# When the next generator in a lane of side work may begin: at its own due time, or as soon as the one ahead of it is through

## The chip, the cores and the metric

The kernel runs on one core of one Trainium2 chip. The metric is the device time of one execution in microseconds; before the change it is 2041.46 us, the median of three runs (2041.38, 2041.46 and 2047.03). The profile shown below is of one further execution, which took 2036.54 us.

The engines are named as the profile names them: PE is TensorE (matmuls and transposes), DVE is VectorE, ACT is ScalarE, POOL is GpSimd and SP is SyncE, which here only issues DMA transfers. Each engine takes its instructions in the order in which they were written, and waits where an operand is not there yet.

## The reference

Two transformer blocks run one after the other on 512 tokens of 1024 features, all in float32. Cut to what matters here:

```
# block 1
x  = x + gate_a * (concat(gla(h), pool(h)) @ w_out)       # w_out: 1024 x 1024
h2 = modulate(rmsnorm(x), ...)
logits = h2 @ [w_router_group, w_router_expert]            # 36 columns
x  = x + gate_m * moe(h2)                                  # 32 experts, two per token
x  = rmsnorm(x)
# block 2, layer A: gated delta rule, 8 heads of 128, chunks of 64 tokens
q, k, v, z, b, a = split(rms_norm(x) @ w_in)
q, k, v = silu(causal_depthwise_conv(q | k | v))           # 4 taps
q, k    = l2_norm(q), l2_norm(k)                           # per head and token
beta = sigmoid(b);  g = -exp(a_log) * softplus(a + dt_bias)
g_cum = cumsum(g in chunks)
a_low = strictly_lower((k * beta) @ k.T * decay(g_cum))
sol   = solve(I + a_low, [v * beta, k * beta * exp(g_cum)])
... scan over the chunks; o = rms_norm(o) * silu(z);  x = x + o @ w_out
x = x + swiglu(rms_norm(x))
# layer B: stick-breaking attention on shared k and v, then swiglu again
```

## The kernel before

The activations lie transposed in SBUF, features on the partitions and all 512 tokens on the free axis. A float32 product is made of three matmuls of halves: the high part of the weights (`ah`, from `whi`) and the low part (`al`) by the high part of the activations, and the high by the low. The profile shows these three as `mm<-ah,whi`, `mm<-al,whi` and `mm<-ah,wlo`, each 128x512. They are the main work of TensorE. `fm_pair` (from L509) makes two output tiles of a projection from 48 such matmuls. The last matmul of a tile is followed at once by an eviction, which `evict` issues (a `scalar_tensor_tensor` or `tensor_tensor` on VectorE, from PSUM to SBUF).

Everything else that a stage needs is side work. It is written as Python generators, and between each group of three matmuls `fm_pair` calls `tick` (L464), which lets side work issue a piece. The side work is kept in eight lanes, called A, I, B, J, C, V, W and X (L408). A lane is a queue of generators: the first of them runs, in pieces, and each piece ends with a `yield`. While it writes the program the kernel keeps an estimate of when each engine would be free and when each tile would be written (`Clock`, `Engine`). Two numbers follow from it for each lane. `add` (L420) stores with a generator the estimated time at which its input is there, `at`. `ready[lane]` is the estimated time at which what the last piece of that lane issued is finished. The larger of the two is the lane's due time:

```
def due(s, lane):
    q = s.lanes[lane]
    return max(s.ready[lane], q[0][1]) if q else 1e30
```

`tick` goes through the lanes and calls `step` once for each lane whose due time is not later than TensorE's estimated time. `until` and `drain`, which empty lanes where a phase ends or a tile is needed, take the lane with the smallest due time instead. `step` (L424) takes the next piece of the lane's first generator. If that generator turns out to have no further piece, it is taken off the queue and the loop goes on with the next generator in the same call. All this is done while the program is written. On the chip there is only the resulting order of instructions on each engine.

Two stretches of the program use the lanes in the way that matters here.

The second half of the out-projection of block 1 (`out(j, 1)`, from L1221; 281 to 320 us in the trace) has eight output tiles, k = 0 to 7. Eviction k (`xT<-mm,modT,xT` on VectorE) adds two generators. `router_gen(k)` in lane C issues the four router matmuls `lC<-wrg,xT` that read the evicted tile. `rows_gen(k)` in lane X issues four transposes `lA<-cst,xT` of it, then a copy on ScalarE (`rows<-lA`), and for k = 3 and 7 a store. The eviction is also squared (`nsq`, ScalarE) and summed (`nacc`, VectorE). `lA<-ones,nacc` on TensorE reads the sum after the last tile. The MoE follows.

The gated delta-net (`gdn`, from L1738; from 597 us) projects k, b and a, q, v and z in the order of `GDN_ORDER`: k0, ba, k1, k2, k3, q0, v0, q1, v1, q2, v2, q3, v3, z0 to z3, where each of these but ba is a pair of heads and 48 matmuls. Each evicted head (`xm<-mm,Rc`, VectorE) goes through `conv_gen` in lane V or W: one tap on ScalarE, three on VectorE (`kF<-xm,vbT,kF`, `qF<-...`, `vf<-...`, 128x512), and a silu on ScalarE. When that is done, it adds a generator to lane C. For a k or q head this is `norm_gen`: a square on ScalarE (`cs<-kF`), its sum on TensorE (`lC<-ones,cs`), and small work on VectorE (`kss`, `qss`). For a v head it is `v_gen`: four transposes `lC<-cst,vf` on TensorE, and `vb<-lC,rho` on VectorE. `gates_gen`, in lane C too, makes beta and the decays of all heads: `lC<-cst,baf`, some small work on VectorE and ScalarE (`beta`, `gm`), then `lC<-gm,cst` on TensorE. `lower` (lanes I and B) makes the triangular matrices from them (`lB<-ub,gm`, `E`, `lB<-kF`). `solve` (lane J) inverts their 32x32 blocks on VectorE in 30 steps of two instructions (`sub<-mt`, `mt<-mt,sub`), and gives way after each four steps. Its result goes through memory (`inv`) to `levels` in lane I (`lB<-inverted,XTs`).

On ScalarE the functions of exp and ln are in one table and silu in another. Where a function of the other table comes next, an ACT_TABLE_LOAD is issued.

Of the kernel before, what the change touches and what calls it, by code (L numbers as in the profile page):

```python
# [263 lines left out]
class Stream:  # L264
# [77 lines left out]
    def next(s, key):  # L342
        i = s.nn
        assert s.items[i][0] == key, (s.items[i][0], key)
        s.nn += 1
        if i - 1 in s.held:
            s.release(*s.held.pop(i - 1))
        with s.K.aside():
            s.split_to(i + 2)
            s.load()  # L350
        return s.hl.pop(i)
# [43 lines left out]
class Kern:  # L395
# [28 lines left out]
    def step(s, lane):  # L424

        q = s.lanes[lane]
        main = s.cur
        while q:
            gen, at = q[0]
            s.cur = max(s.ready[lane], at)  # L430
            try:
                due = next(gen)
            except StopIteration:
                q.pop(0)
                continue
            s.ready[lane] = s.cur + (due or 0.0)
            s.cur = main
            return True
        s.cur = main
        return False  # L440
# [863 lines left out]
    def moe(s):  # L1304
# [103 lines left out]
        tt(out=gates[:, 1], in0=gates[:, 0], in1=e2, op=OP.mult)  # L1408
        place0, step = sm("place0", [4]), sm("step", [4])
        tt(out=step, in0=oh[:, :, 1], in1=oh[:, :, 3], op=OP.add)  # L1410
        ts_(out=place0, in0=step, scalar1=-32.0, scalar2=64.0, op0=OP.mult, op1=OP.add)
        ts_(out=step, in0=place0, scalar1=-2.0, scalar2=None, op0=OP.mult)

        cnt, more, cap = sm("cnt", [NE]), sm("more", [NP]), sm("cap", [NP, 2])
# [1105 lines left out]
```

## Time and profile before

| | |
|---|---|
| median of three runs | 2041.46 us |
| profiled execution | 2036.54 us |
| its span (first to last instruction) | 2034.8 us |
| mean granted clock of TensorE | 0.973 |
| PE busy | 1952.2 us (96%), 10717 instructions |
| PEld busy (weight loads, beside PE) | 1471.0 us (72%) |
| DVE busy | 984.7 us (48%) |
| ACT busy | 750.9 us (37%) |
| POOL busy | 376.0 us (18%) |

The share of busy time says which engine could set the time. The timeline of that engine, instruction by instruction, says where it stood still, and the entry in brackets at the end of a row says for how long and which engine's instruction released it. Nearly all instructions carry the line L231, the helper through which every operation is issued, so that they are told apart by the names of the tiles they write and read.

### The profile page before, as it was taken

What the parts mean: (1) busy time and instruction counts of PE and PEld (TensorE: products, weight loads), DVE (VectorE), ACT (ScalarE), POOL (GpSimd) and SP (SyncE); (2) the same over time, 40 slices, a digit from 0 to 9 for tenths busy, and PEclk for the clock granted to TensorE, in tenths of its full rate; (3) what the DMA queues carried; (4) which work ended last, traced back from release to release, by engine and by line L of the source; (5) the groups of instructions that cost most, each with busy time, mean ns of one, the idle gap of its engine ahead of it and who ended that gap; (6) DMA issues with size and microseconds to landing.
All of it is one profiled execution on the core that took longest, in us unless ns stands there. A gap on an engine that the chain in (4) does not pass through costs nothing.

```text
span 2034.8 us, 26780 instructions
## 1 busy us (share of the span) xinstructions
PE 1952.2 (96%) x10717; PEld 1471.0 (72%) x10717; DVE 984.7 (48%) x1612; ACT 750.9 (37%) x1184; POOL 376.0 (18%) x305
## 2 busy tenths in 40 slices
PE   7999997999997998999999999999999989999999
PEld 4766775344445776888788888888888768888887
DVE  3445433343447679445554433445665544433432
ACT  3443422222235543334343222224666542322322
POOL 1423202112105342122121100101121221100110
PEclk9989997999999998999999999999999999999999
DMA  9213376999951323101223332323211123333332
GB/s 315 75 44 125 113 271 243 421 415 401 404 198 55 110 78 95 46 22 42 87 87 100 97 100 93 94 88 109 73 63 51 54 73 95 98 98 94 93 93 73
DMA packets 175368, 268.86 MB, mean 132 GB/s; under 512 B 24301, under 2 KB 148457, under 8 KB 162697
## 3 DMA queue, kind: packets, MB, share of 16 engines
q1 hardware_dynamic: 152784, 249.28, 35.5%
q10 hardware_dynamic: 19784, 13.40, 2.2%
q0 software_dynamic: 2672, 4.44, 0.6%
q8 instruction: 86, 1.41, 0.3%
q14 instruction: 42, 0.34, 0.1%
HBM read 263.41 MB, written 7.86 MB: 133 GB/s over the span
## 4 chain that ended last, share of the span: by engine, by line
PE 73%; DVE 6%; ACT 2%; issue 1%; POOL 0%; ACTq 0%; DMA 0%; DVEq 0%; POOLq 0%
PE mm L231 57%; PE lA L231 9%; PE lB L231 7%; DVE qF L231 1%; DVE kF L231 1%; DVE sub L231 1%; PE lC L231 1%; DVE xT L231 1%; DVE mt L231 0%; DVE vf L231 0%; ACT ah L231 0%; DVE wlo L231 0%; DVE al L231 0%; DVE nacc L231 0%; ACT whi L231 0%
## 5 line engine op out<-in xcount | busy, mean ns | idle before, releaser
L231 PE MATMUL mm<-ah,whi 128*128 128x512 f32 (+1 forms) x1232 | 503.5, 409 | 0.6 <-DVE xT L231 0.5
L231 PE MATMUL mm<-al,whi 128*128 128x512 f32 (+1 forms) x1232 | 487.9, 396 | 8.6 <-DVE al L231 8.5
L231 PE MATMUL mm<-ah,wlo 128*128 128x512 f32 (+1 forms) x1232 | 487.4, 396 | 0.8 <-DVE wlo L231 0.8
L231 DVE TENSOR_TENSOR wlo<-wraw,whi 128x1024 fp32r<-128x1024 f32 (+3 forms) x174 | 216.1, 1244 | 289.3 <-ACT whi L231 287.9
L231 ACT ACTIVATE whi<-wraw 128x1024 fp32r<-128x1024 f32 (+2 forms) x212 | 214.7, 1014 | 327.8 <-PE mm L231 172.1
L231 PEld LDWEIGHTS mm<-ah,whi 128*128 128x128 f32 (+1 forms) x1232 | 234.3, 190 | 60.4 <-issue 8.9
L231 PEld LDWEIGHTS mm<-al,whi 128*128 128x128 f32 (+1 forms) x1232 | 234.2, 190 | 59.5 <-DVE al L231 11.4
L231 PEld LDWEIGHTS mm<-ah,wlo 128*128 128x128 f32 (+1 forms) x1232 | 233.9, 190 | 54.0 <-DVE wlo L231 2.0
L231 POOL TENSOR_TENSOR sg<-sg,fR 128x512 f32<-128x512 f32 x44 | 57.0, 1298 | 525.5 <-ACT sg L231 525.5
L231 POOL TENSOR_TENSOR wlo<-wraw,whi 128x1024 fp32r<-128x1024 f32 x38 | 94.2, 2480 | 247.8 <-ACT whi L231 242.1
L231 PE MATMUL mm<-hidh,whi 128*128 128x512 f32 x352 | 139.2, 395 | 0.0
L231 PE MATMUL mm<-hidh,wlo 128*128 128x512 f32 x352 | 138.0, 392 | 0.0
L231 PE MATMUL mm<-hidl,whi 128*128 128x512 f32 x352 | 136.6, 388 | 0.0
L231 PE MATMUL mm<-slot,moex 128*32 128x512 f32 (+1 forms) x1024 | 116.8, 598 | 0.1
L231 ACT ACTIVATE moex<-lA,modP,g2P 128x128 f32<-128x128 f32 x64 | 27.5, 455 | 161.1 <-PE lA L231 145.8
L231 PEld LDWEIGHTS mm<-slot,moex 128*32 128x32 f32 x1024 | 31.6, 110 | 71.4 <-issue 64.1
L231 PEld LDWEIGHTS mm<-hidh,wlo 128*128 128x128 f32 x352 | 66.1, 188 | 15.5
L231 PEld LDWEIGHTS mm<-hidl,whi 128*128 128x128 f32 x352 | 66.1, 188 | 14.5
L231 PEld LDWEIGHTS mm<-hidh,whi 128*128 128x128 f32 x352 | 66.2, 188 | 13.0
L231 DVE TENSOR_TENSOR xT<-mm,xT 128x512 f32<-128x512 f32 x64 | 44.0, 687 | 56.2 <-PE mm L231 51.0
L231 ACT ACTIVATE hidh<-fu 128x512 fp32r<-128x512 f32 x44 | 27.8, 633 | 104.3 <-DVE fu L231 104.3
L231 POOL TENSOR_TENSOR nacc<-nacc,nsq 128x512 f32<-128x512 f32 x28 | 39.5, 1409 | 144.7 <-ACT nsq L231 144.7
(552 smaller groups left out, 3104.8 us busy)
## 6 DMA issues: line engine op xcount, KB each, us to landing
slot<-in_w_e_in_dram SPq DMA_DIRECT2D x64, 1024.0 KB, 12.2
wraw<-in_w_gu_dram SPq DMA_DIRECT2D x88, 512.0 KB, 3.4
slot<-in_w_e_out_dram SPq DMA_DIRECT2D x32, 1024.0 KB, 13.3
wraw<-in_w_down_dram SPq DMA_DIRECT2D x40, 512.0 KB, 3.4
wraw<-in_w_ada_dram SPq DMA_DIRECT2D x32, 512.0 KB, 4.1
wraw<-in_gdn_w_in_dram SPq DMA_DIRECT2D x32, 512.0 KB, 3.8
wraw<-in_w_kv_dram SPq DMA_DIRECT2D x16, 512.0 KB, 3.3
wraw<-in_w_in_dram SPq DMA_DIRECT2D x14, 512.0 KB, 4.6
```

The lines of the kernel that those rows point to most:

```text
L231: r = f(*a, **k)
```

## The change

In `step`, when a generator has no further piece and is taken off its lane's queue, the lane now goes on with the next one in the same call only if that generator's own due time is not later than TensorE's estimated time. Otherwise `step` returns, and the next generator begins at a later `tick`, when its time has come.

```
             except StopIteration:
                 q.pop(0)
+                s.cur = main
+                if q and s.due(lane) > s.nc.tensor.t:
+                    return True
                 continue
```

The rule holds for all lanes and the whole program. The order that comes out differs in two stretches alone, the two described above; the rest reads the same on every engine. TensorE, VectorE, GpSimd and SyncE have as many instructions as before, and SyncE's order is unchanged. ScalarE has 1282 instead of 1278. The four that are added are ACT_TABLE_LOADs, all in the gated delta-net.

The first of three places is TensorE in the out-projection of block 1, at the eviction of tile 0, where the router matmuls and the transposes of this tile stand.

```order
L231 MATMUL mm<-ah,whi 128x512
L231 MATMUL mm<-al,whi 128x512
L231 MATMUL mm<-ah,wlo 128x512
L231 MATMUL lC<-wrg,xT 128x36 x4
L231 MATMUL mm<-ah,whi 128x512
L231 MATMUL mm<-al,whi 128x512
L231 MATMUL mm<-ah,wlo 128x512
L231 MATMUL lA<-cst,xT 128x128 x4
```

After the change:

```order
L231 MATMUL mm<-ah,whi 128x512
L231 MATMUL mm<-al,whi 128x512
L231 MATMUL mm<-ah,wlo 128x512
L231 MATMUL mm<-ah,whi 128x512
L231 MATMUL mm<-al,whi 128x512
L231 MATMUL mm<-ah,wlo 128x512
L231 MATMUL lC<-wrg,xT 128x36 x4
L231 MATMUL mm<-ah,whi 128x512
L231 MATMUL mm<-al,whi 128x512
L231 MATMUL mm<-ah,wlo 128x512
```

The router matmuls of a tile no longer stand right behind its last matmul; six matmuls of the next tile come between them, and the other tiles are moved in the same way or further.

The second place is VectorE at the start of the gated delta-net, where the taps of the first k heads (`kF`) and the gates (`beta`, `gm`) share the queue. Before the change:

```order
L231 TENSOR_TENSOR baf<-mm,Rc 16x512
L231 SCALAR_TENSOR_TENSOR kF<-xm,vbT,kF 128x512 x2
L231 TENSOR_SCALAR beta<-beta 128x32
L231 RECIPROCAL beta<-beta 128x32
L231 TENSOR_TENSOR gm<-lC,ab 128x32
L231 SCALAR_TENSOR_TENSOR gm<-gm,nbeta 128x32
L231 SCALAR_TENSOR_TENSOR gm<-gm,ab 128x32
L231 TENSOR_TENSOR gml<-gm,gmh 128x32
L231 SCALAR_TENSOR_TENSOR kF<-xm,vbT,kF 128x512 x3
```

After the change:

```order
L231 TENSOR_TENSOR baf<-mm,Rc 16x512
L231 SCALAR_TENSOR_TENSOR kF<-xm,vbT,kF 128x512
L231 TENSOR_SCALAR beta<-beta 128x32
L231 RECIPROCAL beta<-beta 128x32
L231 TENSOR_TENSOR gm<-lC,ab 128x32
L231 SCALAR_TENSOR_TENSOR gm<-gm,nbeta 128x32
L231 SCALAR_TENSOR_TENSOR gm<-gm,ab 128x32
L231 TENSOR_TENSOR gml<-gm,gmh 128x32
L231 SCALAR_TENSOR_TENSOR kF<-xm,vbT,kF 128x512 x2
L231 MEMSET xm 128x3
L231 TENSOR_TENSOR xm<-mm,Rc 128x512
L231 SCALAR_TENSOR_TENSOR kF<-xm,vbT,kF 128x512 x2
```

One tap instead of two stands ahead of `beta`, and an eviction stands among the taps behind `gml`.

The third place is VectorE near the end of the solve, where the last taps of a q head (`qF`) stand among the batches of `sub` and `mt`. Before the change:

```order
L231 SCALAR_TENSOR_TENSOR qF<-xm,vbT,qF 128x512 x2
L231 TENSOR_TENSOR sub<-mt 128x150
L231 TENSOR_TENSOR mt<-mt,sub 128x6x25
L231 TENSOR_TENSOR sub<-mt 128x130
L231 TENSOR_TENSOR mt<-mt,sub 128x5x26
L231 TENSOR_TENSOR sub<-mt 128x108
L231 TENSOR_TENSOR mt<-mt,sub 128x4x27
L231 TENSOR_TENSOR sub<-mt 128x84
L231 TENSOR_TENSOR mt<-mt,sub 128x3x28
L231 MEMSET xm 128x3
L231 TENSOR_TENSOR xm<-mm,Rc 128x512
```

After the change:

```order
L231 TENSOR_TENSOR sub<-mt 128x150
L231 TENSOR_TENSOR mt<-mt,sub 128x6x25
L231 TENSOR_TENSOR sub<-mt 128x130
L231 TENSOR_TENSOR mt<-mt,sub 128x5x26
L231 TENSOR_TENSOR sub<-mt 128x108
L231 TENSOR_TENSOR mt<-mt,sub 128x4x27
L231 TENSOR_TENSOR sub<-mt 128x84
L231 TENSOR_TENSOR mt<-mt,sub 128x3x28
L231 SCALAR_TENSOR_TENSOR qF<-xm,vbT,qF 128x512 x2
L231 MEMSET xm 128x3
L231 TENSOR_TENSOR xm<-mm,Rc 128x512
```

The last two taps now stand behind a batch of eight solve instructions that they stood ahead of.

How far TensorE's reading of a head stands behind the head's eviction, counted in main matmuls between the two in the program as written, is as follows. The instructions are those of lane C, and the heads count from 0 to 7.

| PE instruction | head | before | after |
|---|---|---|---|
| `lC<-gm,cst` (behind `lC<-cst,baf`) | all | 21 | 27 |
| `lC<-ones,cs` | k2 | 34 | 48 |
| `lC<-ones,cs` | k4 | 62 | 42 |
| `lC<-ones,cs` | q0 | 30 | 27 |
| `lC<-ones,cs` | q3 | 38 | 41 |
| `lC<-cst,vf` | v0 | 38 | 30 |

The first `lB<-kF` stands 18 matmuls behind the `lB<-ub,gm` of its matrices before, and 12 after. The `lC<-cst,vf` of the last two heads, v6 and v7, come 21 and 24 matmuls later in the program than before, with 9 instead of 6 matmuls between the two.

## Rows read from the trace of the kernel before

**Rows 1.** Busy time by window: PE, PEld, DVE, ACT, POOL; clock, DMA share, GB/s.
```profile
280.00:345.00 65.00, 51.91 (x317) 41.55 (x316) 27.71 (x80) 14.76 (x28) 11.22 (x27) 0.84 0.65 243
345.00:597.00 252.00, 250.59 (x1910) 105.59 (x1912) 102.75 (x184) 66.37 (x128) 37.88 (x28) 0.99 0.94 382
...
760.00:820.00 60.00, 51.49 (x260) 41.90 (x258) 53.97 (x102) 20.69 (x28) 14.24 (x6) 0.89 0.35 93
```

**Rows 2.** Timeline, TensorE, out-projection: start, duration, instruction, [idle before <-releaser].
```profile
288.08 0.39 PE L231 MATMUL mm<-al,whi 128*128 128x512 f32 x1
288.31 0.39 PE L231 MATMUL mm<-ah,wlo 128*128 128x512 f32 x1
289.54 1.08 PE L231 MATMUL lC<-wrg,xT 128*128 128x36 f32 x8 [0.84 <-DVE xT L231]
...
294.84 0.63 PE L231 MATMUL lA<-cst,xT 128*128 128x128 f32 x4 [0.94 <-DVE xT L231]
...
318.47 1.08 PE L231 MATMUL lC<-wrg,xT 128*128 128x36 f32 x8 [0.84 <-DVE xT L231]
...
320.01 0.69 PE L231 MATMUL lA<-ones,nacc 128*128 128x2 f32 x5
```

**Rows 3.** Timeline, VectorE, same stretch.
```profile
288.74 0.75 DVE L231 SCALAR_TENSOR_TENSOR xT<-mm,modT,xT 128x512 f32<-128x512 f32 x1 [3.27 <-PE mm L231]
...
319.17 0.69 DVE L231 TENSOR_TENSOR nacc<-nacc,nsq 128x512 f32<-128x512 f32 x1 [0.76 <-ACT nsq L231]
```

**Rows 4.** Timeline, SyncE's queue, before and into the MoE.
```profile
345.76 0.90 SPq L231 DMA_DIRECT2D slot<-in_w_e_out_dram  x2
```

**Rows 5.** Timeline, TensorE, GDN stage: the waits longer than one microsecond, and one slow matmul.
```profile
647.01 1.08 PE L231 MATMUL lC<-gm,cst 128*128 128x32 f32 x8 [2.36 <-DVE gm L231]
...
649.06 0.63 PE L231 MATMUL mm<-ah,whi 128*128 128x512 f32 x1
...
665.39 1.02 PE L231 MATMUL lC<-ones,cs 128*64 128x2 f32 x16 [2.92 <-ACT cs L231]
...
716.36 0.93 PE L231 MATMUL lC<-ones,cs 128*64 128x2 f32 x16 [1.44 <-ACT cs L231]
...
755.29 0.63 PE L231 MATMUL lC<-ones,cs 128*64 128x2 f32 x16 [1.68 <-ACT cs L231]
...
771.85 1.12 PE L231 MATMUL lC<-cst,vf 128*128 128x128 f32 x4 [2.78 <-ACT vf L231]
...
793.87 1.02 PE L231 MATMUL lC<-ones,cs 128*64 128x2 f32 x16 [5.74 <-ACT cs L231]
...
835.77 0.90 PE L231 MATMUL lC<-cst,vf 128*128 128x128 f32 x4 [3.50 <-ACT E L231]
```

**Rows 6.** Timeline, VectorE, GDN stage.
```profile
638.85 5.19 DVE L231 SCALAR_TENSOR_TENSOR kF<-xm,vbT,kF 128x512 f32<-128x512 f32 x2 [0.20 <-ACT kF L231]
643.96 1.25 DVE L231 TENSOR_SCALAR beta<-beta 128x32 f32<-128x32 f32 x1
...
652.67 0.74 DVE L231 SCALAR_TENSOR_TENSOR kF<-xm,vbT,kF 128x512 f32<-128x512 f32 x1
...
791.27 1.41 DVE L231 SCALAR_TENSOR_TENSOR qF<-xm,vbT,qF 128x512 f32<-128x512 f32 x2
792.60 0.30 DVE L231 TENSOR_TENSOR sub<-mt 128x150 f32<-128x150 f32 x1
...
794.83 0.24 DVE L231 TENSOR_TENSOR mt<-mt,sub 128x84 f32<-128x84 f32 x1
```

**Rows 7.** Timeline, GpSimd, beside the first of them.
```profile
638.28 5.20 POOL L231 TENSOR_TENSOR wlo<-wraw,whi 128x1024 fp32r<-128x1024 f32 x2 [8.80 <-ACT whi L231]
```

**Rows 8.** Timeline, ScalarE, GDN stage.
```profile
793.20 0.61 ACT L231 ACTIVATE cs<-qF 128x512 f32<-128x512 f32 x1
...
831.98 1.28 ACT L218 ACT_TABLE_LOAD   x1 [1.92 <-DMA inverted<-inv]
833.27 0.60 ACT L231 ACTIVATE eg<-lB 128x512 f32<-128x512 f32 x1
```

## The prediction

> **What bounds the kernel now.** I read the busy times first. TensorE is busy for 1952.2 of 2034.8 us, VectorE for about half of that. A change of order can only take away what TensorE stands still, some 80 us, and what it loses at a low clock beside that. The order differs in two stretches, so I then read the busy time by window to see how tight they are. From 345 to 597 us, in the MoE, TensorE is busy for 250.6 of 252 us and the DMA engines for 0.94 [rows 1]. From 760 to 820 us, in the delta-net's solve, VectorE is busy for 53.97 us and TensorE for 51.49 of 60 [rows 1]. There the two engines are both near their limit, and VectorE is the nearer. Last I read TensorE's timeline in the two stretches for its idle times and the instruction that ended each.
>
> **The out-projection.** Main matmuls start 0.23 us apart (288.08, 288.31), and the router matmuls behind the last of a tile start 1.23 us after it, at 289.54 [rows 2]. They wait for the eviction, which starts at 288.74 and takes 0.75 us [rows 3]. So such a place costs 1.0 us. There are four of them, at 289.54, 304.01, 312.86 and 318.47 us, each with an idle time of 0.84 us; a fifth is the transposes at 294.84, idle for 0.94, which costs 1.1 [rows 2]. After the change six matmuls, 1.4 us, stand between, more than the 1.0 us that is missing, and the eviction depends on nothing that moves. The first three and the fifth go: 3 × 1.0 + 1.1 = 4.1 us. The place at 318.47 is behind the last tile, where no matmul is left to fill it. The way to `lA<-ones,nacc` at 320.01 leads there through the eviction, the square and the sum at 319.17 [rows 2, 3] in any case, and it keeps its length. About 0.4 us is added to the gain by a set of transposes that moves from among the matmuls into this wait. The sum is −4.5 us, with ends at 0 and −5.
>
> Does it carry? The next transfer of an expert's weights that is issued after the first ones stands at 345.76 us [rows 4], behind work that hangs on the router, so that it starts earlier by what the router does. With TensorE without a gap in the MoE [rows 1], the whole of the stage shifts. I count the 4.5 us in full.
>
> **The delta-net, its start.** TensorE stands 2.36 us before `lC<-gm,cst` at 647.01, and after it eight matmuls show 0.63 us as that at 649.06 does, against 0.39 elsewhere [rows 2, 5]: 8 × 0.24 = 1.9 us at the low one of the two clocks (1.2 instead of 2.4 GHz), which followed the pause. The cause is VectorE. `beta` begins at 643.96, right behind two taps that took 5.19 us together from 638.85 [rows 6], while GpSimd did two `wlo` from 638.28 [rows 7]. Two taps alone take 1.41 us (791.27), so they lost 3.8 us to the overlap [rows 6]. After the change `beta` stands behind one of the two, that is some 2.6 us earlier, and `lC<-gm,cst` six matmuls (1.4 us) later. Together this is 4.0 us against a wait of 2.36; but the small instructions now meet the second `wlo`, which ends at 643.48 [rows 7], and then they start only 0.5 us earlier. I leave 0.5 us of the wait standing: −(2.36 + 1.9 − 0.5) = −3.8 us. The wait for the squares of k head 2 at 665.39 is 2.92 us [rows 5]; they stand 14 matmuls further behind their eviction, 3.2 us, but the taps that they wait for also have a pair of others moved in front of them (1.41). I take −1.2 us (ends 0 and −2.9). The start gives −5.0.
>
> **The middle.** At 716.36 TensorE waits 1.44 us and at 755.29 1.68 us [rows 5]. The squares of q0 and q3 stand 9 and 3 matmuls later in the program. For q0 the wait was on VectorE's queue, and 9 × 0.23 = 2.1 us cover it: −1.4. For q3 3 × 0.23 = 0.7, of which I take −0.5. The ends are 0 and −3.1 for both.
>
> **The solve.** Here VectorE decides. The wait of 2.78 us at 771.85 is for taps of v2 that stand behind the same two batches as before; it stays. The longest wait, 5.74 us at 793.87, is for `cs` at 793.20, behind the silu that follows the taps at 791.27 [rows 5, 6, 8]. These taps now stand behind one batch more. The batch runs from 792.60 to 795.07, so 2.5 us [rows 6], and the square is read three matmuls earlier (0.7): +3.2 us. If such a batch or its taps meet two more `wlo`, they lose 3.8 more, so the ends are 0 (VectorE has one eviction and two taps less among the batches, 0.68 + 2 × 0.7, and three `wlo` may fall otherwise) and +7.0.
>
> **Behind the solve.** TensorE waits 3.50 us at 835.77 for the bank of the transposes of v6 [rows 5]. VectorE frees it behind `E`, which needs `eg` at 833.27, behind a table load at 831.98 of 1.28 us [rows 8]. The transposes stand 24 matmuls later, 5.5 us. I take −3.0 (ends 0 and −3.5).
>
> **New waits.** The squares of k4 come 42 instead of 62 matmuls behind the eviction; k2 had 34 and waited 2.92, so at 8 × 0.23 more cover there remains 1.1. v0's transposes come after 30 instead of 38; q0 at 30 waited 1.44, and I take 1.0. The first `lB<-kF` lose 6 matmuls of cover, 1.4 us, half of it exposed: 0.7. Four more table loads on ScalarE are 4 × 1.28 = 5.1 us [rows 8], most of it beside waiting ScalarE time (busy 20.69 of 60 us in the solve's window [rows 1]); I take 0.2. New waits: +3.0, with ends at 0 and +9.
>
> On the table load the profile shows the next ScalarE instruction at 833.27, 0.01 us behind the load's end [rows 8]. The Trainium skill ("ScalarE: Activation LUTs", section "What ACT_TABLE_LOAD costs") puts a drain of 1380 ns on top of a load of 1283 ns, 2.66 us for each switch. By that rule four loads would come to 10.6 us instead of 5.1, and if they stood on the path the result would be slower. The trace here agrees with the load and shows no drain behind it.
>
> The sum: −4.5 − 5.0 − 1.9 + 3.2 − 3.0 + 3.0 = −8.2 us. From the profiled execution of 2036.54 this gives 2028.3. The median of the three runs lies 4.9 us above that execution, and the runs after will be compared with it, so I predict 2041.46 − 8.2 = 2033.
>
> **The rivals.**
> - *VectorE takes the delta-net's gain back.* Only the out-projection gains. In the solve's window VectorE is busy for 90% [rows 1]; whatever TensorE gains ahead of it, it waits for there, as long as VectorE's work starts no earlier. Against it: the start's gain brings the evictions forward too, and with them VectorE's work. −4.5, with +1 for what the moved batch costs: −3.5, 2038.
> - *All waits go.* The moved taps find VectorE free and GpSimd's `wlo` fall elsewhere. Then the out-projection gives 4.5, the start 2.4 + 1.9 + 2.9 = 7.2, the middle 3.1, the part behind the solve 3.5, with nothing new: −18.3, 2023. For it: each wait is short against the matmuls put before it. Against it: VectorE has no room in the solve.
> - *Slower: the late taps of q4.* The mechanism sits at 793.87. The taps moved behind the last full batch meet two `wlo` there, so that the wait grows by 3.2 + 3.8 = 7.0 us to some 13 us. The low clock follows it for eight matmuls, 1.9 us, as behind 647.01 [rows 5]. What the start and the middle gained is lost in this wait, since VectorE ends it, and the part behind the solve gives nothing, since two of the four added table loads (2 × 1.28 [rows 8]) then fall to the late q heads. The sum is 7.0 + 1.9 + 2.6 − 4.5 = +7.0, 2048. It decides from the point at which the wait at q4's squares is longer than 12 us. In favour: VectorE and GpSimd already meet for 3.8 us at 638.85 [rows 6, 7], and VectorE is the fuller engine here. Against: the moved taps are only two. Of such a meeting the Trainium skill ("SBUF — State Buffer", section "🔬 SBUF: two separate sides") says that GpSimd and a VectorE operation with two SBUF inputs take their shared ports for a whole instruction and block each other. By that rule a tap can lose up to a whole `wlo`, 2.6 us by the row [rows 7] instead of 1.9, and the sum would be +8.4; the 5.19 us for two taps agree with blocking.
>
> **How the numbers follow.** What a measurement of this kernel can tell from no change is about 0.3%, 6.1 us. The forecast, −8 with ±4, gets 0.46, and about 0.32 of it is beyond 6.1 us. The first rival gets 0.23 (−1 to −6.5), nearly all within, 0.03 beyond. The second gets 0.17, all faster. The third gets 0.14, of which 0.12 is beyond 6.1 us. So faster 0.52, same 0.36, slower 0.12. The range goes from 2019, the second rival with two more stretches at the full clock (2 × 1.9), to 2045: the forecast with the upper ends of the solve (3.8) and the new waits (6) and one more stretch at the low clock (1.9). It leaves out most of the third rival and a little beyond the second. The forecast's own range is 2029 to 2037.
>
> **What would show it.** Right: in the out-projection no idle time before `lC<-wrg,xT` save the last, and `lA<-ones,nacc` near 315.5 us; `lC<-gm,cst` with less than 1 us of wait and no slow matmuls behind it; the wait at q4's squares grown to about 9 us; the wait at the last `lC<-cst,vf` gone; the stages behind 900 us as long as before. Wrong: a wait of over 12 us at q4's squares or of over 2 us at k4's; a first wait for weights in the MoE; a delta-net that ends as late as before although its start was early; or a difference of more than 1 us between the parts that were not reordered.

## The result and the profile after

The kernel after takes 2032.48 us, the median of 11 runs (2020.68 to 2040.04), against 2041.38 us for the kernel before in 11 runs beside it (2034.91 to 2047.03). The ratio is 0.995, with a 95% interval from 0.9927 to 0.9972 (here and below it is taken over all runs, and not from the two medians). The medians differ by 9 us, the ratio comes to 10, and the interval goes from 6 to 15 us. The forecast of 2033 us and its sign hold. What stands behind the number is another matter for the delta-net, as the traces and the runs below show.

The page of the kernel after, its first two lines (span, then busy time, share and instructions of each engine):

```profile
span 2027.4 us, 26781 instructions
...
PE 1949.6 (96%) x10717; PEld 1468.5 (72%) x10717; DVE 981.0 (48%) x1612; ACT 756.3 (37%) x1188; POOL 373.8 (18%) x305
```

Here TensorE is as busy as before to within 3 us of 1952, and the four table loads are the 1188 instead of 1184 instructions of ScalarE. The span is 7.4 us shorter. TensorE's standing still, span less busy time, fell from 82.6 to 77.8 us, and nearly all of these 4.8 us are the out-projection's. In the delta-net it hardly changed, as will be seen.

The stages by window, in the kernel after (columns as in [rows 1]):

```profile
345.00:597.00 252.00, 249.48 (x1892) 105.96 (x1891) 100.18 (x182) 64.90 (x126) 38.92 (x29) 0.99 0.96 388
640.00:700.00 60.00, 56.70 (x351) 45.43 (x350) 46.18 (x94) 37.89 (x59) 23.77 (x13) 0.94 0.37 111
700.00:760.00 60.00, 57.80 (x361) 47.62 (x359) 46.69 (x93) 33.63 (x43) 29.94 (x15) 0.97 0.30 78
760.00:820.00 60.00, 47.73 (x243) 38.76 (x242) 51.66 (x103) 20.43 (x27) 12.62 (x5) 0.91 0.34 92
820.00:850.00 30.00, 28.81 (x214) 24.82 (x212) 15.31 (x29) 13.01 (x20) 6.48 (x4) 1.00 0.19 45
850.00:900.00 50.00, 47.94 (x363) 42.45 (x362) 24.50 (x61) 22.07 (x41) 9.30 (x7) 1.00 0.10 22
```

And the same windows of the kernel before, as far as [rows 1] does not have them:

```profile
640.00:700.00 60.00, 54.64 (x319) 44.78 (x318) 43.24 (x87) 35.15 (x55) 23.19 (x13) 0.91 0.36 108
700.00:760.00 60.00, 56.22 (x358) 46.45 (x357) 47.23 (x99) 30.02 (x41) 29.21 (x15) 0.94 0.30 77
820.00:850.00 30.00, 26.50 (x172) 22.95 (x171) 13.39 (x22) 9.50 (x15) 6.49 (x4) 0.94 0.19 45
850.00:900.00 50.00, 48.66 (x358) 43.87 (x357) 23.97 (x60) 18.57 (x36) 6.93 (x6) 0.93 0.07 11
```

The MoE is as tight as before [rows 1], 249.48 of 252 us. What differs in the delta-net is TensorE's granted clock, as a share of the full one, the third figure from the right: 0.91, 0.94, 0.89, 0.94 and 0.93 before, and 0.94, 0.97, 0.91, 1.00 and 1.00 after. TensorE's busy time in the solve's window even fell, from 51.49 to 47.73 us of 60.

TensorE in the out-projection, where the router's matmuls stand, after:

```profile
299.53 0.39 PE L231 MATMUL mm<-ah,wlo 128*128 128x512 f32 x1
299.75 0.97 PE L231 MATMUL lC<-wrg,xT 128*128 128x36 f32 x8
...
323.47 1.08 PE L231 MATMUL lC<-wrg,xT 128*128 128x36 f32 x8 [0.41 <-DVE xT L231]
...
325.01 1.02 PE L231 MATMUL lA<-ones,nacc 128*128 128x2 f32 x8
```

These are the router matmuls of tile 1, the ones at 289.54 in [rows 2]. (The place that is shown with the change as that of tile 0 is this one. Those of tile 0 stood six matmuls behind its last one before the change too, at 285.88, and did not wait.) They follow the main matmul ahead of them at the usual 0.22 us, where it was 1.23 [rows 2]. No others wait, nor do the transposes, save the last, which wait 0.41 us behind the eviction as they had to.

The delta-net's waits on TensorE, after:

```profile
652.09 0.97 PE L231 MATMUL lC<-gm,cst 128*128 128x32 f32 x8
...
661.93 1.02 PE L231 MATMUL lC<-ones,cs 128*64 128x2 f32 x16 [3.30 <-ACT cs L231]
...
748.06 0.63 PE L231 MATMUL lC<-ones,cs 128*64 128x2 f32 x16 [2.20 <-ACT cs L231]
...
775.84 1.11 PE L231 MATMUL lC<-cst,vf 128*128 128x128 f32 x4 [8.88 <-ACT vf L231]
...
783.20 0.63 PE L231 MATMUL lC<-cst,vf 128*128 128x128 f32 x4 [1.71 <-DVE vb L231]
...
794.39 0.63 PE L231 MATMUL lC<-ones,cs 128*64 128x2 f32 x16 [1.67 <-ACT cs L231]
```

Against [rows 5]: `lC<-gm,cst` no longer waits, and neither do k2, q0 and, behind the solve, the last v heads. In their place stand a wait of 3.30 us before k0's squares, which had none, one of 2.20 us at q2, where q3 had 1.68, one of 8.88 us at v2, where there were 2.78, and one of 1.71 us at v3. The wait at q4 fell from 5.74 to 1.67.

### The profile page after: what moved, and what is told of

Read it like the earlier page. It is cut to its first block, busy times and chain, and to the rows that moved or that the text cites. A ratio compares the mean times of both kernels' runs of the same rounds, so it can differ in the third digit from the quotient of the medians.

```text
span 2027.4 us, 26781 instructions
## 1 busy us (share of the span) xinstructions
PE 1949.6 (96%) x10717; PEld 1468.5 (72%) x10717; DVE 981.0 (48%) x1612; ACT 756.3 (37%) x1188; POOL 373.8 (18%) x305
## 3 DMA queue, kind: packets, MB, share of 16 engines
q8 instruction: 86, 1.41, 0.3%
## 4 chain that ended last, share of the span: by engine, by line
PE 73%; DVE 5%; ACT 2%; issue 2%; POOL 1%; DMA 0%; ACTq 0%; POOLq 0%; DVEq 0%
PE mm L231 57%; PE lA L231 9%; PE lB L231 7%; DVE sub L231 1%; DVE xT L231 1%; PE lC L231 1%; DVE qF L231 1%; DVE mt L231 0%; ACT ah L231 0%; DVE kF L231 0%; POOL wlo L231 0%; DVE vf L231 0%; DVE wlo L231 0%; DVE al L231 0%; ACT whi L231 0%
## 5 line engine op out<-in xcount | busy, mean ns | idle before, releaser
L231 DVE TENSOR_SCALAR moex<-lA,g2P,modP 128x128 f32<-128x128 f32 x64 | 25.3, 410 | 85.1 <-ACT moex L231 85.1
```

What stands on the lines that cost most here:

```text
L231: r = f(*a, **k)
```

## Where the time went, stage by stage

One profile of each kernel differs from the other also where the program is the same. To the beginning of the out-projection the main matmuls come in the same order in all kernels of this study, and yet that stretch took between 236.3 and 249.3 us in 14 profiles (236.5 in that of before, 246.2 in that of after). The rows of one window show what differs, first before, then after:

```profile
180.00:200.00 20.00, 20.00 (x145) 15.41 (x144) 14.95 (x19) 7.76 (x14) 6.46 (x3) 1.00 0.35 106
```

```profile
180.00:200.00 20.00, 20.00 (x91) 14.54 (x91) 14.87 (x20) 9.25 (x15) 4.93 (x3) 0.66 0.18 53
```

With a clock of 1.00 from 180 to 200 us the stretch took 236 to 241 us, with 0.58 to 0.73 it took 243 to 249. So I read each stage by itself, from the same instruction to the same instruction, and not the sum. The out-projection (its first main matmul to `lA<-ones,nacc`) took 83.5 us before and 78.8 after. In the profiles of all kernels of this study it took 77.9 to 81.8 us in the ten with the new rule there, and 83.1 to 85.3 us in the four without. From there to the first gates matmul it was 319.2 and 320.4 us: what the out-projection gained was handed on. From the first gates matmul to the 1000th main matmul after the out-projection, which lies in the next stage, it was 448.4 and 434.8 us. This last one is called the delta-net's time from here on. Its mark is not quite the same in all orders: in that of after the gates matmul itself stands three main matmuls, 0.7 us, later in the stage. From the stage's first main matmul it is 486.3 and 474.0 us, so that the delta-net became shorter by 12.3 us and not by 13.6, and 0.7 of the 1.2 us by which the stretch ahead of it grew is the mark.

## The experiments

**Each stretch alone.** In both kernels the new condition holds only where a list of lanes, `own`, says so; it is all lanes or none, and set anew before the delta-net. At the end of the MoE all estimates of the planner are moved by a constant, so that the delta-net's order is exactly that of before in the first kernel, and that of after in the second.

```
-                if q and s.due(lane) > s.nc.tensor.t:
+                if q and lane in s.own and s.due(lane) > s.nc.tensor.t:
...
+    K.own = ""          # first kernel; all lanes in the second, none in block 1
     K.gdn()
```

> The new rule holds in block 1 alone, and the planner's estimates are set back to those of before when block 1 and the MoE are through, so that the delta-net's order is that of before. Theory of the prediction: the out-projection loses its four recoverable waits, -4.5 us (the profile after showed -4.8 there), and the MoE hands that on, so the time is 4 to 5 us below before, and the delta-net's own duration is that of before within 1 us. Rival (the MoE's weight transfers give it back): the out-projection ends 4.8 us earlier, but the MoE is longer by as much; no change in all.

Measured: 2034.69 us against 2040.36 us, ratio 0.996 (0.9941 to 0.998). The out-projection took 79.2 us and the delta-net 445.2. The forecast's term of 4.5 us for the out-projection holds, and the MoE did not give it back. The delta-net's time, expected within 1 us of before, differs by 3: for a stage whose order is the same, 445.2 against 448.4 us tells how far two profiles of one order lie apart.

> The new rule holds from the delta-net on alone, and the estimates are set to those after, so that the delta-net's order is that of after and block 1's that of before. The prediction's sum: -3.7 us in the delta-net. From the two profiles: -13 us from the first gates matmul to its end. Rival (VectorE takes it back): 0 to +1 us.

Measured: 2030.51 us against 2040.36 us, ratio 0.9944 (0.9922 to 0.9966), which is 10 us and at least 7. The out-projection took 83.8 us and the delta-net 435.5. The forecast's −3.7 us for the delta-net was too small by a factor of nearly three, and the rival by which VectorE takes all back falls.

**The same rule, planned from other estimates.** The change shortens the out-projection in the planner's own estimates too, by 3.85 us, and the delta-net is then planned from there. Two kernels separate this from the rule: without the constant above, the rule in block 1 alone, and in the delta-net alone.

```
     K.block1()            # third kernel: all lanes here, none below
     K.moe()
+    K.own = ""            # fourth kernel: none above, all lanes here
     K.gdn()
```

> The new rule holds in block 1 alone; the delta-net is planned without it, but from estimates that begin 3.85 us earlier, which moves its order too. If the rule makes the delta-net's gain, only the -4.8 us of the out-projection remain, give or take 3 us for the other order. If the gain came from being planned from other estimates, it is here as well: -15 to -18 us.

Measured: 2034.22 us, ratio 0.9963 (0.994 to 0.9985). In the one profile the delta-net took 438.7 us, 8 less than the mean of the two with the order of before (446.8), and 7 less without the three main matmuls of the mark, although the rule did not hold there. The runs do not bear this out. Their median is only 0.5 us below that of the first kernel, which has the order of before, and −15 to −18 us lie outside the interval (−12 to −3). By the runs the first expectation is met.

> The new rule holds from the delta-net on alone, planned from the estimates of before; its order differs from that of after. If the rule makes the gain, -8 to -13 us here too. If it hangs on the estimates from which the stage is planned, the result is within 3 us of before.

Measured: 2036.69 us, ratio 0.9971 (0.9949 to 0.9992). This is 4 us below before (interval −10 to −2), between the two expectations. In the one profile the delta-net took 439.7 us, 7 less than before, with the rule but from the old estimates. So by single profiles, counted from the stage's first main matmul, the estimates by themselves give 7 us and the rule by itself 7, and both together 10.6 (the mean of after and the second kernel), not 14. By the medians of the runs it is 0.5, 4 and 10 us, each good to some 4. How the gain divides between the rule and the estimates stays open.

The forecast's own step at the start of the delta-net can be followed in these two. VectorE and TensorE in the third kernel, which has no rule in the delta-net:

```profile
644.92 2.25 DVE L231 SCALAR_TENSOR_TENSOR kF<-xm,vbT,kF 128x512 f32<-128x512 f32 x1
647.10 2.37 DVE L231 TENSOR_SCALAR beta<-beta 128x32 f32<-128x32 f32 x1
```

```profile
652.89 0.97 PE L231 MATMUL lC<-gm,cst 128*128 128x32 f32 x8
```

And in the fourth, which has it:

```profile
651.53 4.95 DVE L231 SCALAR_TENSOR_TENSOR kF<-xm,vbT,kF 128x512 f32<-128x512 f32 x2
656.41 1.27 DVE L231 TENSOR_SCALAR beta<-beta 128x32 f32<-128x32 f32 x1
```

```profile
659.48 1.08 PE L231 MATMUL lC<-gm,cst 128*128 128x32 f32 x8 [1.86 <-DVE gm L231]
```

One tap instead of two stands ahead of `beta` in the kernel without the rule, and two in the one with it, and the wait before `lC<-gm,cst` is gone in the former and 1.86 us in the latter. The price that the forecast put on that step was fair. But it is not the rule within the delta-net that brings it about: it comes from the estimates having moved. The long waits of the solve go with the estimates too. The third kernel, without the rule there, waits at v2 as the kernel after does, and the fourth, with it, much as the kernel before does:

```profile
777.98 1.11 PE L231 MATMUL lC<-cst,vf 128*128 128x128 f32 x4 [8.88 <-ACT vf L231]
```

```profile
774.74 1.11 PE L231 MATMUL lC<-cst,vf 128*128 128x128 f32 x4 [2.88 <-ACT vf L231]
...
796.77 1.02 PE L231 MATMUL lC<-ones,cs 128*64 128x2 f32 x16 [6.50 <-ACT cs L231]
```

**Two more pairs.** The delta-net planned without and with the rule, from estimates 1.3 and 2.6 us later than those of before, with the rule in block 1 in all four.

```
+        d = <estimate of before + 1.3 or + 2.6> - s.cur
+        for e in engines + [s.nc.sync]:
+            e.t += d
```

> The rule holds in block 1 alone; the delta-net is planned without it, from estimates 1.3 us later than those of before. Durations are from the first gates matmul to the same matmul of the next stage: 448.4 us in the profile of before, 434.8 in that of after. If the order of before was an unlucky one and the rule brings little, this takes 436 to 441 us. If the rule makes the gain, 445 to 450 us.

> The rule holds throughout; the delta-net is planned with it, from estimates 1.3 us later than those of before. If the rule makes the gain, 434 to 440 us from the first gates matmul to the same matmul of the next stage, and 4 us or more less than without it. If it is the estimates that matter, the same as without it within 2 us.

> As the run without the rule in the delta-net, from estimates 2.6 us later than those of before. Its order has two table loads more than before's, not four. If the order of before was an unlucky one: 436 to 441 us; if the rule makes the gain: 445 to 450 us.

> As the run with the rule throughout, from estimates 2.6 us later than those of before; two table loads more than before's. If the rule makes the gain: 434 to 440 us and 4 us or more less than without it. If it is the estimates: within 2 us of the run without it.

Measured, with all of the above, one profile each: the delta-net's time; TensorE's idle time in the 270 us from the first gates matmul; and the clock lost, which is the sum of (1 − granted clock) × 20 us over the 15 windows of 20 us from there. At the low clock the granted share is 0.50 (before, from 666 to 671 us), so that TensorE stood at the low clock for twice the time in this column.

| rule in the delta-net | estimates | us | idle | clock lost |
|---|---|---|---|---|
| no | before (kernel before) | 448.4 | 22.8 | 20.6 |
| no | before (first kernel) | 445.2 | 24.3 | 15.8 |
| yes | before | 439.7 | 22.1 | 12.0 |
| no | after | 438.7 | 23.9 | 14.0 |
| yes | after (kernel after) | 434.8 | 21.0 | 10.4 |
| yes | after (second kernel) | 435.5 | 22.7 | 8.6 |
| no | + 1.3 us | 439.3 | 21.5 | 14.0 |
| yes | + 1.3 us | 443.6 | 22.9 | 17.2 |
| no | + 2.6 us | 448.9 | 26.0 | 20.6 |
| yes | + 2.6 us | 435.3 | 20.6 | 8.8 |

By pairs the rule is worth −7.1, −3.6, +4.3 and −13.6 us, −5 in the mean, with a spread larger than that. Of the expectations, "an unlucky order" holds for + 1.3 and falls for + 2.6; "the rule makes the gain" falls for + 1.3 and holds for + 2.6, and "the same within 2 us" falls for both. What the rule does to the delta-net in general is thus not settled by four pairs, most of them of single profiles. What they show is that this kernel's gain there is one draw among eight orders, which differ by up to 14 us; about 3 us of such a difference can be the scatter of profiles of one order.

The two right columns say what the draw decides. The idle time is nearly the same in all orders, 20.6 to 26.0 us. The clock lost goes from 8.6 to 20.6 us, and the delta-net's time goes with it: 434.8 to 435.5 us for 8.6 to 10.4, 438.7 to 439.7 for 12.0 to 14.0, 443.6 to 445.2 for 15.8 to 17.2, and 448.4 to 448.9 for 20.6. It is longer by about 1.2 us for each us of clock lost. The time less the idle time less the clock lost is 401 to 406 us in all ten rows, so that these two account for all but some 5 us of the differences. The order alone does not decide the clock: the two profiles with the order of before lost 20.6 and 15.8 us. What the traces show of how this comes about: in the kernel before, six stretches of main matmuls take 0.63 us each, behind the waits at 647.01, 665.39, 716.36, 771.85, 793.87 and 835.77 [rows 5], 52 matmuls in all. In the kernel after there are three, from 662.9, 749.9 and 776.6 us, with 28. A seventh stretch of the kernel before, from 873.48 us, holds small matmuls behind the solve, which in the kernel after run at the full clock; first before, then after:

```profile
873.48 2.06 PE L231 MATMUL lA<-vn,kd 64*128 64x128 f32 x8
```

```profile
869.78 1.16 PE L231 MATMUL lA<-vn,kd 64*128 64x128 f32 x8
```

The wait of 8.88 us at v2 is followed by one such stretch of 4.2 us, as that of 2.78 us was by one of 5.5. The long wait thus cost no more slow main matmuls than the short one, and the idle time stayed nearly the same while the waits over 1.4 us went from seven to five.

This is read from single profiles. Of the runs, the span and the mean granted clock are on record, and so for each the clock lost in the whole kernel, (1 − granted clock) × span, and the rest of its span. The means, in us:

| kernel | runs | clock lost | rest |
|---|---|---|---|
| before (beside the four) | 35 | 55.0 | 1985.1 |
| first (out-projection alone) | 12 | 51.5 | 1981.6 |
| second (delta-net alone) | 12 | 48.6 | 1981.6 |
| third | 12 | 54.5 | 1977.3 |
| fourth | 12 | 53.9 | 1980.7 |
| after | 11 | 53.3 | 1976.1 |

The standard error is 1.0 to 2.1 us for the clock lost and below 1 us for the rest. The second kernel bears the reading out: 6.4 of its 10 us are clock lost. The kernel after does not: it lost 1.7 us less than before, good to 5, and 9 us of its gain are in the rest (of the 11 runs of before beside it no clock is on record, so the 35 stand for them). The clock lost ahead of the out-projection alone goes from 11 to 24 us in the 14 profiles, which blurs such a sum. So the clock's share in the gain of the kernel after is open.

**The overlap at the start.** The kernel before, and the kernel after, with the six `wlo` of the k pairs written by a copy on ScalarE in place of GpSimd's subtraction (so their values are other ones); the planner still counts the subtraction. In effect:

```
-            e.tensor_tensor(out=l, in0=x, in1=h.bitcast(F), op=OP.subtract)   # GpSimd
+            nc.scalar.activation(l, x, AF.Copy)                               # for gk only
```

> The kernel before, with the low parts of the k pairs' weights (six wlo) written by a plain copy on ScalarE instead of the subtraction on GpSimd, so that their values are other ones; the order is else the same, and ScalarE has six times 1.04 us more. Theory (VectorE's taps lose their time to GpSimd's wlo): the two taps ahead of beta take 1.4 instead of 5.2 us, TensorE's wait of 2.36 us before the gates' sums goes with the slow matmuls behind it, and from the first gates matmul to main matmul 168 of the stage it takes 31 to 33 instead of 35.5 to 37.1 us. Rival (the chain through beta is too long by itself): the wait stays above 1.5 us.

VectorE and TensorE in this kernel:

```profile
643.53 1.41 DVE L231 SCALAR_TENSOR_TENSOR kF<-xm,vbT,kF 128x512 f32<-128x512 f32 x2 [1.14 <-ACT kF L231]
646.73 1.30 DVE L231 TENSOR_SCALAR beta<-beta 128x32 f32<-128x32 f32 x1 [1.79 <-ACT beta L231]
```

```profile
649.83 1.08 PE L231 MATMUL lC<-gm,cst 128*128 128x32 f32 x8 [1.44 <-DVE gm L231]
```

The two taps take 1.41 us, as [rows 6] has it for two taps alone, so the 5.19 us were the overlap. The wait shrinks to 1.44 us only, because `beta` now stands behind ScalarE's copies, but k2's wait of 2.92 us is gone too. Against the expectation, eight slow matmuls still follow, from 652.0 us. To main matmul 168 of the stage it takes 30.0 us, against 37.1 and 35.5. By one profile the overlap costs the start 5 to 7 us, which is the forecast's sum for it (5.0) by another split.

> The kernel after, with the same replacement of the six wlo by a copy on ScalarE. Theory (the new wait of 3.30 us before the squares of k0 comes from two taps that took 3.89 us beside a wlo): it falls to below 1 us. Rival (it comes from the table load of 1.28 us, which now stands ahead of k0's silu): it stays above 2 us.

```profile
648.58 1.02 PE L231 MATMUL lC<-ones,cs 128*64 128x2 f32 x16 [2.90 <-ACT cs L231]
```

```profile
644.34 1.28 ACT L231 ACT_TABLE_LOAD   x1
645.63 0.63 ACT L231 ACTIVATE kF<-kF 128x512 f32<-128x512 f32 x1
...
646.78 0.61 ACT L231 ACTIVATE kF<-kF 128x512 f32<-128x512 f32 x1
...
647.91 0.61 ACT L231 ACTIVATE cs<-kF 128x512 f32<-128x512 f32 x1
```

The wait before k0's squares is still 2.90 us. The expectation falls: the taps' overlap does not make it. From `lC<-gm,cst` to k0's squares it takes 9.84 us in the kernel after (652.09 to 661.93). In the kernel before it took as long, 9.68 us from 647.01, without a wait:

```profile
656.69 0.63 PE L231 MATMUL lC<-ones,cs 128*64 128x2 f32 x16
```

The chain between the two is one and the same: the exponentials of the gates, the table load of 1.28 us, k0's silu, its square. Before, 30 main matmuls stood in it, eight of them at the low clock; after, 24, all at the full clock. What TensorE gained at `lC<-gm,cst` it thus waits for, in part, at k0. The rival is met by its number and names a link of that chain, but not what changed. The delta-net took 437.8 us in this kernel, 3 more than after: the overlap gone, nothing was gained there.

**The solve.** The kernel after, with each solve instruction on VectorE computing one row only (the inverse is then another one), in the same order.

```
-    tt(out=tmp, in0=mt[:, j + 1:, j:j + 1]..., in1=mt[:, j:j + 1, 0:j]..., op=OP.mult)
+    tt(out=tmp[:, 0:1], in0=mt[:, j + 1:j + 2, j:j + 1]..., in1=mt[:, j:j + 1, 0:j], op=OP.mult)
```

> The kernel after, with each of the 60 solve instructions on VectorE computing one row only (about 0.19 instead of 0.35 us), so that the inverse is another one; the order is the same. Theory (VectorE's batches end the waits at v2 and q4): the four batches ahead of v2's last tap take 5 us less, and the wait there falls from 8.88 to about 4 us, that at q4 to nothing. Rival (they hang on ScalarE or on evictions): the wait at v2 stays above 7 us.

```profile
765.86 1.12 PE L231 MATMUL lC<-cst,vf 128*128 128x128 f32 x4 [4.08 <-ACT vf L231]
```

The wait at v2 falls to 4.08 us and q4 does not wait, as expected. VectorE's batches ahead of the taps end these waits. In this one profile the delta-net takes 430.8 us, 4 less than after.

The kernel after, with the solve giving way after two steps instead of four:

```
-                if j % 4 == 0:
+                if j % 2 == 0:
                     yield
```

> The kernel after, with the solve giving way after every two steps instead of four, so that the taps of a head stand behind shorter batches; v2's last tap then stands behind 8 steps of the solve, not 16. If the batches ahead of the taps make the wait, it falls from 8.9 to about 3 us, and the delta-net from the first gates matmul to the same matmul of the next stage takes 428 to 431 us instead of 435: 5 us faster than after. If VectorE as a whole is the bound there, the wait only moves to a later head: 433 to 437 us.

```profile
771.65 0.65 PE L231 MATMUL lC<-cst,vf 128*128 128x128 f32 x4 [2.03 <-ACT vf L231]
...
829.65 0.63 PE L231 MATMUL lC<-cst,vf 128*128 128x128 f32 x4 [1.80 <-DVE qss L231]
...
832.03 1.92 PE L231 MATMUL lB<-inverted,XTs 128*128 128x128 f32 x8
834.64 1.16 PE L231 MATMUL lB<-XTs,inverted 128*128 128x128 f32 x8 [0.69 <-ACT XTs L231]
...
838.48 1.16 PE L231 MATMUL lB<-XTs,inverted 128*128 128x128 f32 x8 [0.69 <-ACT XTs L231]
...
843.15 0.33 PE L231 MATMUL lB<-ub,gmh 128*128 128x128 f32 x1 [2.62 <-ACT wq L231]
```

Measured: 2033.95 us against 2040.8 us, ratio 0.9971 (0.9946 to 0.9995), and in its profile the delta-net takes 444.3 us, 9 more than after. By the runs the two kernels cannot be told apart (2032.48 us after). The wait at v2 falls to 2.03 us, better than expected, and main matmul 600 of the stage comes after 167.3 us instead of 176.3. Behind it all is lost: the solve's last instruction ends at 812 instead of 795 us, `lB<-inverted,XTs` begins at 832.03 instead of 813.37, and the steps that hang on the inverse then wait for each other with few main matmuls left to put between them. By the profile that is worse than either expectation. The wait did not grow, it moved: TensorE's idle time is 20.9 us, against 21.0 after, but the clock lost is 17.2 us, against 10.4. No version of this study beats the kernel after by more than the measurement can tell.

## Why the prediction was right, and where it was not

- **The out-projection (−4.5).** Right in place, size and cause: 83.5 to 78.8 us in the profiles, and the first kernel of the experiments has it alone. The MoE hands it on. `lA<-ones,nacc` came at 325.01 and not near 315.5 us, since everything ahead of the out-projection took 9.7 us longer. The prediction named a difference of over 1 us between the parts that were not reordered as a sign of being wrong; here the order was the same and the granted clock was not.
- **The start of the delta-net (−5.0).** Right in size: to main matmul 168 it took 37.1 us before (35.5 in the second profile of the order) and 30.3 after; from the stage's first main matmul it is 5.5 us less. The price of the overlap is confirmed. That the tap ahead of `beta` moves with the estimates, and not with the rule in the delta-net, the prediction did not ask. It is incomplete too: the waits before `lC<-gm,cst` and k2 are both gone, more than was forecast, and k0's wait of 3.30 us was not seen coming.
- **The middle (−1.9).** q0's wait is gone as the sum had it; q3's of 1.68 became one of 2.20 at q2, behind which a stretch at the low clock came as the one behind q0 went.
- **The solve (+3.2).** This step failed. "It stays", the prediction said of the wait of 2.78 us at 771.85, with v2's taps "behind the same two batches as before"; both are wrong, and so is a wait at q4 of about 9 us. v2's first tap stood ahead of the second batch before (757.03) and stands behind it after (762.37), so that its last one now stands behind one batch more; in the kernel after:

```profile
773.61 0.41 DVE L231 TENSOR_TENSOR sub<-mt 128x240 f32<-128x240 f32 x1
774.06 0.41 DVE L231 TENSOR_TENSOR mt<-mt,sub 128x240 f32<-128x240 f32 x1
774.38 1.41 DVE L231 SCALAR_TENSOR_TENSOR vf<-xm,vbT,vf 128x512 f32<-128x512 f32 x2
```

  The wait at v2 became 8.88 us, and behind it q4 had time: 1.67. The waits of the solve together went from 8.5 to 12.3 us (with 1.71 at v3), +3.8 against the +3.2 of the sum, so the amount was right by luck and the place wrong. The rival of late q4 taps did not occur for the same reason. As the third and fourth kernels show, the wait at v2 grew with the estimates and not with the rule.
- **Behind the solve (−3.0).** The wait of 3.50 us is gone, and with it a stretch at the low clock.
- **New waits (+3.0).** Those priced, at k4, v0 and the first `lB<-kF`, did not come; one of 3.30 at k0 did. On the table loads the kernel after shows the same as before, no pause behind the load:

```profile
657.69 1.28 ACT L231 ACT_TABLE_LOAD   x1
658.98 0.63 ACT L231 ACTIVATE kF<-kF 128x512 f32<-128x512 f32 x1
```

  The Trainium skill's drain ("ScalarE: Activation LUTs", "What ACT_TABLE_LOAD costs") shows in neither trace: in both the next instruction follows the load by 0.01 us. The two orders from estimates 2.6 us later have 31 loads each (before 29, after 33) and are the slowest and one of the fastest, so that the loads do not decide.
- **The sum.** The forecast had −8.2 us, −3.7 of it in the delta-net: −1.8 of idle time and −1.9 at the low clock. In the two profiles the idle time there did fall by 1.8 us, in part by luck, since the waits at k0 and v2 grew where no such growth was forecast. The mis-sized term is the low clock, which the sum priced at one place of six (1.9 us): the clock lost in the delta-net fell by 10 us between the two profiles. By stages the profiles give −4.7 and −12.3, or −10.6 by the means of two. These add to −15 to −17, the median moved by −8.9 (interval −15 to −6), and the two halves measured alone by −5.7 and −9.9. Whether the difference is the scatter of the first 240 us is left open; it alone spans 13 us. The runs bear out the share of the clock for the second kernel and not for the kernel after. So the number came out right with a delta-net term too small, and only part of its reasons were.

## What to carry to other kernels

Where TensorE's clock falls behind each pause, count the pauses and the slow stretches behind them, not only the sum of the idle time: here eight orders of one stage, with idle times within 6 us of each other, differed by 14 us in their profiles. Then look at all runs too: a stage that is 8 us shorter in one profile (the third kernel) need not be so in twelve runs. A rule in a planner acts also by moving the estimates from which later stages are planned, so that a gain in a later stage is put down to the rule only after it was seen from other estimates too, with and without the rule. And before an instruction is moved away from a wait, see who reads the same chain next: what TensorE no longer waited before `lC<-gm,cst` it waited, in part, before the squares of k0, since the chain between the two takes 9.7 us in either order.

## What was not expected of the hardware

The same order of main matmuls took 236.3 to 249.3 us up to the out-projection, with a granted clock of 1.00 or of 0.58 to 0.73 from 180 to 200 us. And a wait of 8.88 us was followed by nine matmuls of 0.63 us, one of 2.78 us by twelve.
